# Down projections of a two-layer decoder trunk: three of the seven block products accumulate onto the first one's PSUM banks

## The chip, the cores and the metric

The kernel runs on one core of one Trainium2 chip. The metric is the device time of one execution in microseconds (us); the median of three runs of the kernel before is 2087.05 us (2086.24 to 2087.7).

## The reference, cut to what matters

The model is a trunk of two layers over 1024 tokens with 1024 features, all in float32: a short gated convolution with a feed-forward block, then latent attention with a feed-forward block, and a last RMS norm. The change touches the second half of both feed-forward blocks, the down projection with the 2816 x 1024 matrix `w2`, and the operands that are made for it:

```python
def swiglu_ffn(h, w13, w2):
    g, u = jnp.split(h @ w13, 2, axis=-1)
    return (jax.nn.silu(g) * u) @ w2
...
h = h + swiglu_ffn(rms_norm(h, conv_ffn_norm_g[i]), conv_ffn_w13[i], conv_ffn_w2[i])
...
h = h + swiglu_ffn(rms_norm(h, mla_ffn_norm_g[j]), mla_ffn_w13[j], mla_ffn_w2[j])
```

## The kernel before, in words

Every matrix product splits its two operands into a high and a low part (`split`, L109: ScalarE casts to the high part, VectorE subtracts it to get the low part) and multiplies high by high, high by low and low by high (`three`, L152): three matmuls, lines 153, 154 and 155, per tile of 128 x 128 weights and 512 tokens. In the profile the matmul of L153 reads `mp_hi` and `wp_hi`, that of L154 `mp_lo` and `wp_hi`, that of L155 `mp_hi` and `wp_lo`.

The large products use a Strassen scheme with seven block products in place of eight. For the down projection (`Down`, L658) the contraction (22 chunks of 128) and the output features (8 blocks of 128) and the tokens (1024) are each cut in half. A product `i` of the seven takes one half-size weight block (read from `w2`, or a sum of such blocks that GpSimd's queue has put into DRAM earlier) and one half-size operand (from `md`, in DRAM). It runs over 11 chunks in six groups, five of two chunks and one of one chunk. A step is one chunk: four banks `q` (one per 128 output features), three matmuls each, 12 matmuls. So a product is 11 steps and 132 matmuls, and a down projection is seven products. Two of them run in the kernel, "the first" (L1190) and "the second" (L1701).

For each group there is a load of `m` and of `w` on SyncE's queue (7 or 8 steps ahead) and `parts` (L693), which makes the high and low parts of both: ScalarE `mp_hi`, VectorE `mp_lo`, ScalarE `wp_hi`, VectorE `wp_lo`. `parts` is put two steps ahead of the group's first step (L714). The high tiles share four buffers (`hi_tile`), and so do the low tiles, which holds two groups; a third group's parts wait for the first group's matmuls.

The result `st.h` has 8 blocks of features and two halves of tokens; the four pairs of halves are written (cb, t). Each product has a list of outputs with signs in the table `SEVEN` (L647): after the product, `evict` (L738) adds or subtracts each bank into each listed part of `st.h`, one VectorE instruction of 128 x 512 from PSUM (line 740). There are 14 such pairs in the table, 4 instructions each. They are spread two to a step over the steps that follow the product (`s + j // 2`, L745). `LAST` (L656) names the product after which a part of `st.h` is final, and two steps later `complete` hands it to what follows.

The order of work is written out by hand: `Steps` (L266) holds the steps, and what is put before or after a step is emitted there. Within an engine's queue that is the order of execution. What is put after a step is emitted ahead of what is put before the next one. Each product allocates four of PSUM's eight banks in its first step, so a product's banks were last read by the additions of the product two places earlier.

In the first down projection VectorE also computes the rotary tables (`tables`, L1112, one small piece per step; the profile calls their tiles `rot`), and in its last products `raw_parts` (L1168) splits the finished parts of `st.h`. In the second one `finish` (L1641) squares and scales the finished parts, and the last product is done in halves of 256 tokens.

Before the down projection, `ffn_quads` (L1007) makes the seven operands from pairs of blocks; `right` (L1034) makes operand 6 and `corner` (L1042) makes operand 4 with VectorE subtractions of 128 x 512 (line 1047).

Of the kernel before, what the change touches and what calls it, by code (L numbers as in the profile page):

```python
# [13 lines left out]
ALU = mybir.AluOpType  # L14
# [34 lines left out]
def trunk(ctx, tc, aps, out):  # L49
    nc = tc.nc  # L50
# [199 lines left out]
    class Stream:  # L250


        def __init__(self):
            self.h = [None] * KD
            self.acc = None
# [282 lines left out]
    def complete(n, t, final, keep=True):  # L538

        final(n, t)  # L540
        if t and keep:
            nc.sync.dma_start(hd[n], st.h[n])
# [89 lines left out]
    class Kept:  # L632
# [11 lines left out]

    SEVEN = (  # L647
# [7 lines left out]
    )  # L655
    LAST = {(0, 0): 3, (1, 0): 4, (0, 1): 5, (1, 1): 6}  # L656

    class Down:  # L658


        def __init__(self, steps, m, ws, nk, w, final, keep=True, half=None):

            self.by_half = half
            self.m, self.ws, self.half, self.final, self.keep = m, ws, nk // 2, final, keep
            self.groups = [list(range(a, min(a + 2, self.half))) for a in range(0, self.half, 2)]
            self.wv = w.rearrange("(k p) n -> p k n", p=P)
            self.ends = []
            for i in range(7):
                self.product(steps, i)

        def product(self, steps, i):
            wb, mb, outs = SEVEN[i]
            banks, tail = [], []
            for g, ks in enumerate(self.groups):
                n = len(ks) * 512
                box = {}

                def load_m(box=box, ks=ks, n=n):
                    box["m"] = slot("m")[:, :n]
                    nc.sync.dma_start(box["m"].rearrange("p (k t) -> p k t", t=512),  # L680
                                      self.m[mb - 1, ks[0]:ks[-1] + 1].rearrange("k p t -> p k t"))

                def load_w(box=box, g=g, ks=ks, n=n):
                    r = box["w"] = raw_tile("w2")[:, :n]
                    if isinstance(wb, int):
                        nc.sync.dma_start(r, self.ws[wb, g][:, :n])
                    else:
                        cb, kb = wb
                        k = kb * self.half + ks[0]
                        nc.sync.dma_start(r.rearrange("p (k m) -> p k m", m=512),  # L690
                                          self.wv[:, k:k + len(ks), cb * 512:(cb + 1) * 512])

                def parts(box=box, n=n):  # L693
                    for key in ("m", "w"):
                        hi, lo = hi_tile(key + "p_hi")[:, :n], lo_tile(key + "p_lo")[:, :n]
                        split(hi, lo, box[key])
                        box[key + "p"] = (hi, lo)

                def one(c, q, ts=slice(0, 512), box=box, ks=ks):
                    if not banks:  # L700
                        banks.extend(ps1("dn") for _ in range(4))
                    k = ks[c]
                    (mh, ml), (wh, wl) = box["mp"], box["wp"]
                    cs, ws = slice(c * 512 + ts.start, c * 512 + ts.stop), slice(c * 512 + q * P, c * 512 + (q + 1) * P)
                    more = {"skip_group_check": True} if ts.start else {}
                    three(banks[q][:, ts], wh[:, ws], wl[:, ws], mh[:, cs], ml[:, cs], k == 0, k == self.half - 1, **more)

                s = len(steps.pe)
                if i == 0 and g == 0:
                    self.start = s  # L710
                    steps.before(s, lambda: load_h((4, 5, 6, 7, 0, 1, 2, 3)))
                steps.before(max(s - 8, self.start + 2) if g == len(self.groups) - 1 else s - 8, load_m)
                steps.before(s - 7, load_w)
                steps.before(s - (1 if tail else 2), parts)  # L714
                if i == 6 and g >= len(self.groups) - 2:
                    tail += [lambda q, *ts, c=c, one=one: one(c, q, *ts) for c in range(len(ks))]
                    continue
                for c in range(len(ks)):
                    s = steps.add(lambda c=c, one=one: [one(c, q) for q in range(4)])
            if tail and self.by_half:  # L720
                halves = [slice(th * 256, (th + 1) * 256) for th in range(2)]

                def add(q, th):
                    hv = st.h[4 + q][:, 512:][:, halves[th]]
                    nc.vector.tensor_tensor(hv, hv, banks[q][:, halves[th]], ALU.add)

                for th in range(2):
                    for q in range(4):
                        s = steps.add(lambda q=q, th=th: [fn(q, halves[th]) for fn in tail])
                        steps.after(s, lambda q=q, th=th: self.by_half(q, th, lambda: add(q, th)))  # L730
                self.ends.append(s)
                return
            for q in range(4 if tail else 0):
                s = steps.add(lambda q=q: [fn(q) for fn in tail])
            self.ends.append(s)
            todo = [(q, *o) for q in range(4) for o in outs]

            def evict(q, cb, t, sign):  # L738
                hv = st.h[cb * 4 + q][:, t * 512:(t + 1) * 512]
                nc.vector.tensor_tensor(hv, hv, banks[q], ALU.add if sign > 0 else ALU.subtract)  # L740
                if LAST[cb, t] == i and tail:
                    complete(cb * 4 + q, t, self.final, self.keep)

            for j, o in enumerate(todo):
                n = s - 3 + o[0] if tail else s + j // 2  # L745
                steps.after(n, lambda o=o: evict(*o))
                if LAST[o[1], o[2]] == i and not tail:
                    steps.after(n + 2, lambda o=o: complete(o[1] * 4 + o[0], o[2], self.final, self.keep))

    class Norm:  # L750

# [255 lines left out]
    def ffn_quads(w13, m):  # L1007
        wv = w13.rearrange("a k n -> (a k) n").rearrange("(k p) n -> p k n", p=P)

        first = {}  # L1010

        def store(i, j, t):
            nc.sync.dma_start(m[i - 1, j], t)

        def one(j):

            last, j0, box = j >= KF // 2, j % (KF // 2), {}

            def product(c1, c2):
                nc.vector.tensor_tensor(c1, c1, c2, ALU.mult)  # L1020
                store(2 if last else 1, j0, c1[:, :512])
                if last:
                    store(3, j0, c1[:, 512:])
                    box["b"] = [(c[:, :512], c[:, 512:]) for c in (first.pop(j0), c1)]
                else:
                    first[j] = c1

            def left(c1, c2):
                (b11, b12), (b21, b22) = box["b"]
                box["s"] = work("msum")  # L1030
                box["t1"], box["t2"] = box["s"][:, :512], box["s"][:, 512:]
                sub(5, box["t1"], b12, b11)

            def right(c1, c2):  # L1034
                (b11, b12), (b21, b22) = box["b"]
                sub(6, box["t2"], b22, box["t1"])

            def low(c1, c2):
                (b11, b12), (b21, b22) = box["b"]
                sub(7, b12, b22, b12)  # L1040

            def corner(c1, c2):  # L1042
                (b11, b12), (b21, b22) = box["b"]
                sub(4, b21, box["t2"], b21)

            def sub(i, o, x, y):
                nc.vector.tensor_tensor(o, x, y, ALU.subtract)
                store(i, j0, o)

            done = [product, left, right, low, corner] if last else [product]  # L1050
            return Quad(wv, j * P, DFF + j * P, AF.Silu, done, nc.vector)

        return [one(j + f) for j in range(KF // 2) for f in (0, KF // 2)]
# [48 lines left out]
    e = pl.ends  # L1102
# [92 lines left out]
    for j, fn in enumerate(turns_[0] + turns_[1]):  # L1195
        steps.before(dn.start + 6 + j, fn)
    for j in range(4):
        steps.before(e[3] + 3 + 2 * j, lambda n=j: raw_parts(n, 0))
        steps.before(e[4] + 3 + 2 * j, lambda n=j + 4: raw_parts(n, 0))
        steps.before(e[5] + 3 + 2 * j, lambda n=j: raw_parts(n, 1))  # L1200


# [548 lines left out]
```

## Time and profile before

| | value |
|---|---|
| median of three runs | 2087.05 us |
| the profiled execution's own time | 2084.46 us |
| its span, first to last instruction | 2082.7 us |
| TensorE matmul busy | 98 % of the span |
| VectorE busy | 70 % |
| ScalarE busy | 41 % |
| mean granted TensorE clock | 0.999 of full speed |
| first down projection | 771 to 985 us |
| second down projection | 1852 to 2072 us |

A matmul's row lasts longer than its share of the pipeline: consecutive matmuls start closer together than one lasts. So a lost moment on TensorE is read from the distance between two starts, not from a busy share. In the timeline a row gives the start, the duration, the engine, the line, the operation and its tiles; a bracket at its end gives the idle time before it and what ended that time.

### The profile page before, as it was taken

What the parts mean: (1) busy time and instruction counts of PE and PEld (TensorE: products, weight loads), DVE (VectorE), ACT (ScalarE), POOL (GpSimd) and SP (SyncE); (2) the same over time, 40 slices, a digit from 0 to 9 for tenths busy, and PEclk for the clock granted to TensorE, in tenths of its full rate; (3) what the DMA queues carried; (4) which work ended last, traced back from release to release, by engine and by line L of the source; (5) the groups of instructions that cost most, each with busy time, mean ns of one, the idle gap of its engine ahead of it and who ended that gap; (6) DMA issues with size and microseconds to landing.
All of it is one profiled execution on the core that took longest, in us unless ns stands there. A gap on an engine that the chain in (4) does not pass through costs nothing.

```text
span 2082.7 us, 25559 instructions
## 1 busy us (share of the span) xinstructions
PE 2050.6 (98%) x9542; PEld 1701.2 (82%) x9542; DVE 1463.8 (70%) x2201; ACT 855.4 (41%) x1441; POOL 267.4 (13%) x388
## 2 busy tenths in 40 slices
PE   7999999999999999999999999999999999999998
PEld 6888888888888887787788888788888888888887
DVE  5996666787666667967577777637986666667555
ACT  7533434533333333354345545325533333333355
POOL 1111100121121210000023222110111111100000
PEclk9999999999999999999999999999999999999999
DMA  7255765596766687554332213525487475686543
GB/s 236 81 135 138 237 240 174 118 215 182 190 162 158 145 267 269 197 207 143 87 74 69 53 56 92 190 86 179 135 199 180 147 171 151 153 301 219 182 167 127
DMA packets 274317, 338.98 MB, mean 163 GB/s; under 512 B 18047, under 2 KB 177984, under 8 KB 273872
## 3 DMA queue, kind: packets, MB, share of 16 engines
q1 hardware_dynamic: 240144, 262.71, 38.8%
q0 software_dynamic: 33888, 74.56, 16.7%
q8 instruction: 75, 1.23, 0.2%
q14 instruction: 50, 0.41, 0.1%
q10 hardware_dynamic: 160, 0.07, 0.0%
HBM read 260.22 MB, written 126.35 MB: 186 GB/s over the span
## 4 chain that ended last, share of the span: by engine, by line
PE 88%; DVE 6%; ACT 3%; issue 2%; DMA 2%; DVEq 0%; SPq 0%; ACTq 0%
PE q L153 16%; PE q L155 16%; PE q L154 16%; PE dn L155 5%; PE dn L154 5%; PE dn L153 5%; PE ps_s L1480 4%; PE pl L155 2%; PE pl L153 2%; PE pl L154 2%; PE ps_t L1502 1%; DVE wp_lo L112 1%; PE ps_l L155 1%; PE ps_l L153 1%; PE ps_l L154 1%
## 5 line engine op out<-in xcount | busy, mean ns | idle before, releaser
L153 PE MATMUL q<-xh,w_hi 128*128 128x512 f32 x1568 | 612.5, 391 | 0.7 <-ACT c L451 0.4
L154 PE MATMUL q<-xl,w_hi 128*128 128x512 f32 x1568 | 610.6, 389 | 0.7 <-DVE xl L963 0.7
L155 PE MATMUL q<-xh,w_lo 128*128 128x512 f32 x1568 | 610.3, 389 | 0.0
L153 PEld LDWEIGHTS q<-xh,w_hi 128*128 128x128 f32 x1568 | 294.3, 188 | 63.8 <-ACT xh L959 0.9
L154 PEld LDWEIGHTS q<-xl,w_hi 128*128 128x128 f32 x1568 | 294.4, 188 | 63.0 <-DVE xl L963 1.9
L155 PEld LDWEIGHTS q<-xh,w_lo 128*128 128x128 f32 x1568 | 294.3, 188 | 61.1
L112 DVE TENSOR_TENSOR w_lo<-wr,w_hi 128x512 fp32r<-128x512 f32 (+1 forms) x272 | 191.9, 706 | 199.6 <-ACT w_hi L111 197.8
L111 ACT CAST w_hi<-wr 128x512 fp32r<-128x512 f32 (+1 forms) x272 | 170.1, 629 | 292.6 <-DVE wr L390 196.2
L155 PE MATMUL dn<-mp_hi,wp_lo 128*128 128x512 f32 (+1 forms) x628 | 244.0, 388 | 2.5 <-DVE wp_lo L112 0.8
L153 PE MATMUL dn<-mp_hi,wp_hi 128*128 128x512 f32 (+1 forms) x628 | 242.8, 387 | 0.0
L154 PE MATMUL dn<-mp_lo,wp_hi 128*128 128x512 f32 (+1 forms) x628 | 242.1, 386 | 0.0
L1083 POOL COPY paced<-pace 128x1 f32<-128x1 f32 x128 | 73.0, 570 | 999.7 <-ACT pace L1082 999.7
L112 DVE TENSOR_TENSOR mp_lo<-m,mp_hi 128x1024 fp32r<-128x1024 f32 x84 | 95.3, 1135 | 120.4 <-ACT mp_hi L111 120.4
L111 ACT CAST mp_hi<-m 128x1024 fp32r<-128x1024 f32 x84 | 82.2, 978 | 222.0 <-PE dn L154 211.9
L155 PEld LDWEIGHTS dn<-mp_hi,wp_lo 128*128 128x128 f32 x628 | 117.9, 188 | 32.6 <-DVE wp_lo L112 9.4
L154 PEld LDWEIGHTS dn<-mp_lo,wp_hi 128*128 128x128 f32 x628 | 118.0, 188 | 23.6
L153 PEld LDWEIGHTS dn<-mp_hi,wp_hi 128*128 128x128 f32 x628 | 118.0, 188 | 23.2 <-DVE h L740 0.2
L112 DVE TENSOR_TENSOR wp_lo<-w,wp_hi 128x1024 fp32r<-128x1024 f32 x84 | 94.8, 1129 | 0.0
L473 ACT ACTIVATE c<-c 128x512 f32<-128x512 f32 x44 | 27.8, 633 | 131.9 <-DVE c L448 131.9
L111 ACT CAST wp_hi<-w 128x1024 fp32r<-128x1024 f32 x84 | 81.7, 972 | 0.0
L382 DVE TENSOR_TENSOR w_lo<-wr,w_hi 128x1024 fp32r<-128x1024 f32 x56 | 68.3, 1219 | 12.9 <-ACT w_hi L378 7.9
L1487 ACT ACTIVATE p<-ps_s,mx,rq 128x128 f32<-128x128 f32 (+3 forms) x64 | 53.2, 833 | 53.1 <-DVE mx L1484 47.9
(296 smaller groups left out, 3227.7 us busy)
## 6 DMA issues: line engine op xcount, KB each, us to landing
m<-md_f SPq DMA_DIRECT2D x70, 512.0 KB, 4.8
md_f<-c SPq DMA_DIRECT2D x110, 256.0 KB, 3.7
wr<-in_conv_ffn_w_dram SPq DMA_DIRECT2D x47, 512.0 KB, 6.6
wr<-in_mla_ffn_w_dram SPq DMA_DIRECT2D x47, 512.0 KB, 5.5
w<-mw_f SPq DMA_DIRECT2D x40, 512.0 KB, 3.8
h<-hd SPq DMA_DIRECT2D x32, 512.0 KB, 9.0
wr<-in_conv_w_in_dram SPq DMA_DIRECT2D x31, 512.0 KB, 5.9
mw_f<-in_conv_ffn_w_dram POOLq DMA_DIRECT2D x30, 512.0 KB, 7.5
```

What stands on the lines that cost most here:

```text
L111: nc.scalar.copy(out=hi, in_=src)
L112: (eng or nc.vector).tensor_tensor(lo, src, hi.bitcast(F32), ALU.subtract)
L153: nc.tensor.matmul(ps, lhsT=wh, rhs=xh, start=st, stop=False, **more)
L154: nc.tensor.matmul(ps, lhsT=wh, rhs=xl, start=False, stop=False, **more)
L155: nc.tensor.matmul(ps, lhsT=wl, rhs=xh, start=False, stop=en, **more)
L382: nc.vector.tensor_tensor(lo, self.ra, hi.bitcast(F32), ALU.subtract)
L473: nc.scalar.activation(self.C1[:, 512:], self.C1[:, 512:], self.first)
L1083: nc.gpsimd.tensor_copy(b, a)
L1480: nc.tensor.matmul(ps[:, a:b], lhsT=q[:, qs], rhs=k[:, a:b], start=i == 0, stop=i == 4)
L1487: nc.scalar.activation(p[:, :kw], ps[:, :kw], AF.Exp, bias=mx, scale=rq[:, qb:qb + 1], accum_out=rsum)
L1502: nc.tensor.transpose(t[:, j * P:(j + 1) * P], ps_[j][:, kb * P:(kb + 1) * P], ident)
```

## The change

The table `SEVEN` gets a new order and a flag. Products 2, 3 and 4 (the third, fourth and fifth in time) accumulate on top of product 0 in the same four banks: they take over the list of banks that product 0 left in `self.chain` and don't start a new accumulation. Product 1 runs between product 0 and product 2 in four other banks, products 5 and 6 have banks of their own. Because a bank now holds the sum of product 0 and of those that follow it, each of the first five products has a single output, product 5 has two and product 6 one: eight pairs in place of fourteen, 32 additions per down projection in place of 56. After products 2 and 3 all four additions are emitted right after the last step (`s`), after the others two to a step as before. Operands 4 and 6 change their sign for it; `corner` uses `scalar_tensor_tensor` in place of `tensor_tensor`. `LAST` and the order of `raw_parts` follow the new table: part (1, 0) is final after product 1, part (0, 0) after product 4. The parameters `lag` and `ahead` have the values 2 and 8 that stood there as constants.

```diff
     SEVEN = (
-        ((1, 0), 1, ((1, 0, 1), (1, 1, 1), (0, 0, -1), (0, 1, -1))),
-        (1, 6, ((1, 1, -1), (0, 0, 1), (0, 1, 1))),
-        (3, 7, ((0, 0, -1), (0, 1, -1))),
-        ((0, 1), 4, ((0, 0, -1),)),
-        ((1, 1), 2, ((1, 0, 1),)),
-        (0, 5, ((1, 1, -1), (0, 1, 1))),
-        (2, 3, ((1, 1, 1),)),
+        ((1, 0), 1, False, ((1, 0, 1),)),
+        ((1, 1), 2, False, ((1, 0, 1),)),
+        (1, 6, True, ((1, 1, 1),)),
+        (3, 7, True, ((0, 1, -1),)),
+        ((0, 1), 4, True, ((0, 0, -1),)),
+        (0, 5, False, ((1, 1, -1), (0, 1, 1))),
+        (2, 3, False, ((1, 1, 1),)),
     )
-    LAST = {(0, 0): 3, (1, 0): 4, (0, 1): 5, (1, 1): 6}
+    LAST = {(1, 0): 1, (0, 0): 4, (0, 1): 5, (1, 1): 6}
...
-            wb, mb, outs = SEVEN[i]
-            banks, tail = [], []
+            wb, mb, onto, outs = SEVEN[i]
+            banks, tail = self.chain if onto else [], []
+            if i == 0:
+                self.chain = banks
...
-                    more = {"skip_group_check": True} if ts.start else {}
-                    three(banks[q][:, ts], wh[:, ws], wl[:, ws], mh[:, cs], ml[:, cs], k == 0, k == self.half - 1, **more)
+                    more = {"skip_group_check": True} if ts.start or onto else {}
+                    three(banks[q][:, ts], wh[:, ws], wl[:, ws], mh[:, cs], ml[:, cs], k == 0 and not onto,
+                          k == self.half - 1, **more)
...
-                n = s - 3 + o[0] if tail else s + j // 2
+                n = s - 3 + o[0] if tail else s if i in (2, 3) else s + j // 2
...
-                sub(6, box["t2"], b22, box["t1"])
+                sub(6, box["t2"], box["t1"], b22)
...
-                sub(4, b21, box["t2"], b21)
+                nc.vector.scalar_tensor_tensor(b21, box["t2"], -1.0, b21, ALU.mult, ALU.subtract)
+                store(4, j0, b21)
...
-        steps.before(e[3] + 3 + 2 * j, lambda n=j: raw_parts(n, 0))
-        steps.before(e[4] + 3 + 2 * j, lambda n=j + 4: raw_parts(n, 0))
+        steps.before(e[3] + 3 + 2 * j, lambda n=j + 4: raw_parts(n, 0))
+        steps.before(e[4] + 3 + 2 * j, lambda n=j: raw_parts(n, 0))
```

## Rows read from the trace of the kernel before

**Rows 1.** The page: busy time of each engine (PEld: TensorE's weight loads) with its share of the span and number of instructions, and the granted clock in 40 slices, in tenths.

```profile
PE 2050.6 (98%) x9542; PEld 1701.2 (82%) x9542; DVE 1463.8 (70%) x2201; ACT 855.4 (41%) x1441; POOL 267.4 (13%) x388
...
PEclk9999999999999999999999999999999999999999
```

**Rows 2.** The page: the chain that ended last, shares of the span by engine.

```profile
PE 88%; DVE 6%; ACT 3%; issue 2%; DMA 2%; DVEq 0%; SPq 0%; ACTq 0%
```

**Rows 3.** The instructions that touch the tile `dn` (the banks of both down projections): number, shortest, median and longest duration in ns; then who ended idle time ahead of them (us in total, times).

```profile
L153 PE MATMUL dn<-mp_hi,wp_hi x628: 278/389/482, 771.0 to 2071.5; 128*128 128x512 f32 x151, 128*128 128x256 f32 x6
...
L740 DVE TENSOR_TENSOR h<-h,dn x108: 677/680/690, 803.0 to 2047.9; 128x512 f32<-128x512 f32 x108
...
  DVE wp_lo L112: 10.2, 20
...
  DVE h L740: 0.2, 1
```

**Rows 4.** VectorE in the stretch 770 to 990 us, groups by line and shape: number, busy us, mean ns of one, idle us before them.

```profile
L112 DVE TENSOR_TENSOR mp_lo<-m,mp_hi 128x1024 fp32r<-128x1024 f32 x34 | 41.6, 1223 | 39.1 <-ACT mp_hi L111 39.1
L112 DVE TENSOR_TENSOR wp_lo<-w,wp_hi 128x1024 fp32r<-128x1024 f32 x34 | 41.4, 1218 | 0.0
L740 DVE TENSOR_TENSOR h<-h,dn 128x512 f32<-128x512 f32 x55 | 35.1, 681 | 0.1
L1137 DVE SCALAR_TENSOR_TENSOR rot<-rot 128x512 f32<-128x512 f32 x24 | 16.5, 686 | 0.1
...
L1047 DVE TENSOR_TENSOR msum<-c,msum 128x512 f32<-128x512 f32 x1 | 0.7, 686 | 0.0
```

**Rows 5.** ScalarE's timeline: the cast that opens the preparation of the next product's first group, ahead of the change from product 2 to product 3 of the first down projection.

```profile
860.94 1.05 ACT L111 CAST mp_hi<-m 128x1024 fp32r<-128x1024 f32 x1 [4.30 <-PE dn L154]
```

**Rows 6.** TensorE's timeline: the first matmuls of products 0 and 1 of the first down projection; the first four of its product 3; the first of its product 4; the first of products 3 and 4 of the second down projection.

```profile
770.98 0.39 PE L153 MATMUL dn<-mp_hi,wp_hi 128*128 128x512 f32 x1
...
800.89 0.39 PE L153 MATMUL dn<-mp_hi,wp_hi 128*128 128x512 f32 x1
...
863.69 0.39 PE L153 MATMUL dn<-mp_hi,wp_hi 128*128 128x512 f32 x1
863.91 0.39 PE L154 MATMUL dn<-mp_lo,wp_hi 128*128 128x512 f32 x1
864.44 0.50 PE L155 MATMUL dn<-mp_hi,wp_lo 128*128 128x512 f32 x1
864.78 0.39 PE L153 MATMUL dn<-mp_hi,wp_hi 128*128 128x512 f32 x1
...
894.04 0.39 PE L153 MATMUL dn<-mp_hi,wp_hi 128*128 128x512 f32 x1
...
1942.76 0.39 PE L153 MATMUL dn<-mp_hi,wp_hi 128*128 128x512 f32 x1
...
1973.13 0.39 PE L153 MATMUL dn<-mp_hi,wp_hi 128*128 128x512 f32 x1
```

**Rows 7.** VectorE's timeline at the same four changes of product (2 to 3 and 3 to 4 in the first, then in the second down projection); where a row holds several instructions, its duration is from the first one's start to the last one's end.

```profile
862.02 1.23 DVE L112 TENSOR_TENSOR mp_lo<-m,mp_hi 128x1024 fp32r<-128x1024 f32 x1 [3.48 <-ACT mp_hi L111]
863.17 1.22 DVE L112 TENSOR_TENSOR wp_lo<-w,wp_hi 128x1024 fp32r<-128x1024 f32 x1
864.30 1.41 DVE L1137 SCALAR_TENSOR_TENSOR rot<-rot 128x512 f32<-128x512 f32 x2
865.63 1.28 DVE L740 TENSOR_TENSOR h<-h,dn 128x512 f32<-128x512 f32 x2
...
894.77 0.42 DVE L1153 TENSOR_SCALAR rot<-rot 64x512 f32<-64x512 f32 x1
895.23 1.28 DVE L740 TENSOR_TENSOR h<-h,dn 128x512 f32<-128x512 f32 x2
...
1943.37 1.28 DVE L740 TENSOR_TENSOR h<-h,dn 128x512 f32<-128x512 f32 x2
...
1946.84 2.47 DVE L740 TENSOR_TENSOR h<-h,dn 128x512 f32<-128x512 f32 x4
...
1973.74 1.28 DVE L740 TENSOR_TENSOR h<-h,dn 128x512 f32<-128x512 f32 x2
```

**Rows 8.** Who waited for whom among TensorE's weight loads in 803 to 831 us (first row, inside product 1) and in 834 to 862 us (second row, inside product 2): us in total, times, longest. Then TensorE's timeline at the longest of these places, its weight load first.

```profile
PEld dn L155 <- DVE wp_lo L112: 1.0, 2, 0.5
...
PEld dn L155 <- DVE wp_lo L112: 1.5, 2, 0.8
...
850.40 0.19 PEld L155 LDWEIGHTS dn<-mp_hi,wp_lo 128*128 128x128 f32 x1 [0.78 <-DVE wp_lo L112]
...
849.65 0.39 PE L154 MATMUL dn<-mp_lo,wp_hi 128*128 128x512 f32 x1
850.40 0.50 PE L155 MATMUL dn<-mp_hi,wp_lo 128*128 128x512 f32 x1 [0.36 <-DVE wp_lo L112]
850.74 0.39 PE L153 MATMUL dn<-mp_hi,wp_hi 128*128 128x512 f32 x1
```

**Rows 9.** The longest wait of TensorE for VectorE, at the kernel's start (TensorE's timeline), and the two stretches around and after it (us, then busy us and number of TensorE's matmuls, its weight loads, VectorE, ScalarE and GpSimd, then the granted clock, the DMA share and GB/s).

```profile
13.09 0.67 PE L949 MATMUL xps<-ident,xt 128*128 128x128 f32 x3 [2.20 <-DVE xt L921]
...
10.00:15.00 5.00, 2.63 (x21) 2.06 (x20) 4.39 (x13) 3.25 (x6) 1.66 (x2) 1.00 1.11 359
15.00:20.00 5.00, 4.03 (x17) 2.12 (x15) 3.68 (x7) 4.59 (x8) 0.00 (x0) 1.00 1.02 401
```

More of the change, by code (lines that the diff above doesn't have):

```diff
@@ L647, in trunk, with __init__ @@
     SEVEN = (
[7 rows of a table removed]
+        ((1, 0), 1, False, ((1, 0, 1),)),
[5 more added lines that the diff above has]
+        (2, 3, False, ((1, 1, 1),)),
     )
-    LAST = {(0, 0): 3, (1, 0): 4, (0, 1): 5, (1, 1): 6}
+    LAST = {(1, 0): 1, (0, 0): 4, (0, 1): 5, (1, 1): 6}
     class Down:
-        def __init__(self, steps, m, ws, nk, w, final, keep=True, half=None):
+        def __init__(self, steps, m, ws, nk, w, final, keep=True, half=None, lag=2, ahead=8):
+            self.lag, self.ahead, self.chain = lag, ahead, None
             self.by_half = half
@@ L711, in product @@
                     steps.before(s, lambda: load_h((4, 5, 6, 7, 0, 1, 2, 3)))
-                steps.before(max(s - 8, self.start + 2) if g == len(self.groups) - 1 else s - 8, load_m)
+                steps.before(max(s - self.ahead, self.start + 2) if g == len(self.groups) - 1 else s - self.ahead, load_m)
                 steps.before(s - 7, load_w)
@@ L744, in product @@
             for j, o in enumerate(todo):
-                n = s - 3 + o[0] if tail else s + j // 2
+                n = s - 3 + o[0] if tail else s if i in (2, 3) else s + j // 2
                 steps.after(n, lambda o=o: evict(*o))
                 if LAST[o[1], o[2]] == i and not tail:
-                    steps.after(n + 2, lambda o=o: complete(o[1] * 4 + o[0], o[2], self.final, self.keep))
+                    steps.after(n + self.lag, lambda o=o: complete(o[1] * 4 + o[0], o[2], self.final, self.keep))
     class Norm:
```

## The prediction

> **What bounds the kernel now.** I read the page first. TensorE is busy for 98% of the span, its granted clock is at full speed in every slice [rows 1], and it makes up 88% of the chain that ended last [rows 2]. So the time is the number of matmuls by the distance of their starts, plus the moments in which TensorE has to wait. The change leaves the matmuls alone, and takes work from VectorE. That is worth something only where TensorE waits for VectorE today, and it costs something where TensorE will have to wait anew.
>
> Next I asked who waits at the banks of the down projections. In both together TensorE's idle time is put down to the split `wp_lo` twenty times, and to the additions (line 740) once, for 0.2 us [rows 3]. So the additions are not waited for directly; they stand in VectorE's queue ahead of splits that are. Then I went through TensorE's starts. Between the first matmuls of products 0 and 1 lie 800.89 - 770.98 = 29.91 us for 132 matmuls, 0.227 us each [rows 6]; a larger distance is lost time.
>
> Two kinds of loss come out. The first is at the change of product. The new product's third matmul, L155, starts 0.53 us after the second and the next one 0.34 us after that, which loses 0.53 + 0.34 - 2 x 0.227 = 0.42 us [rows 6]; 0.11 of it is the second distance, a slow restart. The reason is the buffers. The last group has one chunk, one step of 2.7 us. Only when TensorE has left the group before it does ScalarE begin the casts (860.94, after a wait for a matmul) [rows 5]; VectorE's two splits follow at 862.02 and 863.17, and the second ends at 864.39, 0.05 us before L155 starts [rows 6, 7]. VectorE was idle for 3.48 us ahead of them [rows 7], so fewer additions don't bring them forward: this loss stays at every change of product.
>
> The second kind is inside products 1 and 2 of the first down projection, where additions, rotary pieces and splits pile up: four waits of the weight load of L155, 1.0 + 1.5 us [rows 8]. At the longest the load waits 0.78 us and the starts lose 0.75 + 0.34 - 0.45 = 0.64, so 0.14 less. In all 2.5 - 4 x 0.14 = 1.9 us are lost. In the second down projection, without rotary pieces, I find none of this kind.
>
> **What the change removes.** 24 additions per down projection, 48 in all. Four in a row take 2.47 us and one takes 0.68, so they start (2.47 - 0.68)/3 = 0.60 us apart [rows 3, 7]: some 29 us of VectorE, nearly all beside TensorE's work. What is worth time is the pile-up: product 0 leaves 4 additions in place of 16, product 1 leaves 4 in place of 12. I take all 1.9 us as gained; the lower end is 0, should rotary pieces and splits alone be late.
>
> **What it adds.** Product 3 writes onto banks from which product 2's partial sum must first be read, with nothing between the two products, and product 4 onto those of product 3: two handovers per down projection. The new wait stands at the first matmul of each bank. Behind it on TensorE is the whole next product, and behind that ScalarE's next casts, which wait for buffers. When is the addition of bank 0 done? VectorE takes its work in the order written: splits of the next product's first group (put ahead of the last step), rotary pieces, and only then the additions (put after the last step). Today's rows show that order [rows 7].
>
> - First down projection, 2 to 3: the addition starts at 865.63, ends 0.68 later, and with the 0.05 us from above the matmul starts at 866.36 in place of 863.69, 2.67 us late. Add 0.11 for the restart and take off the 0.42, which the longer wait covers: +2.36. Two rotary pieces (1.41 us, from 864.30) stand ahead of it.
> - 3 to 4: 895.23 + 0.73 = 895.96 against 894.04: 1.92 + 0.11 - 0.42 = +1.61. Here one rotary piece is ahead, at 894.77.
> - Second down projection, 2 to 3: 1943.37 + 0.73 = 1944.10 against 1942.76: 1.34 + 0.11 - 0.42 = +1.03.
> - 3 to 4: 1973.74 + 0.73 = 1974.47 against 1973.13, also +1.03, from the same rows [rows 6, 7].
>
> The sum is 6.0 us. Banks 1 to 3 add nothing: the additions follow 0.60 us apart, TensorE takes 3 x 0.227 = 0.68 us per bank. Nor does the next group: its splits now follow four additions, from 865.63 + 3 x 0.60 + 0.68 = 868.1 and end 1.15 + 1.22 later at 870.5, while TensorE needs them 24 matmuls and two after its restart, at 866.36 + 0.11 + 26 x 0.227 = 872.4. No row shows a matmul that waits for an addition of its own bank, so bounds: from below 0 each (the addition is done in time, and the 0.42 stays), from above the same figures plus 3 x 0.60 = 1.8 each, if all four additions had to be done. I take bank 0's own, as the additions are one instruction per bank.
>
> A rule speaks against the change here. The Trainium skill (PSUM — Partial Sum Buffer, "PSUM bank collisions raise a hardware error") says that TensorE and VectorE may not touch one bank at the same moment, and that a bank, not an address, is to be guarded. By the trace alone, where line 740 holds TensorE for 0.2 us in 108 additions, the handover would cost nothing; by the rule it costs the full wait. No run here shows a bank refilled while it is read, since today the banks alternate.
>
> Another rule would make it cheaper: the Trainium skill (TensorE: Matmul & The Clock Gate, the table of specifications at its head) say that TensorE's queue pulls weight loads ahead of matmuls in flight. Then the 0.11 us of restart would fall away at a handover, where weights are ready, and the sum would be 0.44 us less. At today's change of product the weights themselves are late [rows 6], so no row here decides it.
>
> **What costs nothing.** The subtraction that becomes `scalar_tensor_tensor` takes 686 ns in that form on 128 x 512 and 686 as it is [rows 4], 22 times. The signs change no count. Products 1 to 3 load other operands and weights in a new order, as many and as far ahead; each is needed no earlier than it was made before. The finishing of (1, 0) moves from product 4 to product 2, that of (0, 0) from product 3 to product 4, where the other one stood: same work in the same kind of place, and no wait on it in either [rows 3]. Product 5 finds the four banks of product 1, free since early in product 2.
>
> **The sum.** 6.0 - 1.9 = +4.1 us. The profiled execution took 2084.46 us (its span of 2082.7 and 1.8 around it), and would take 2088.6; the median of the runs was 2.6 us above that execution, and carried onto it the forecast is 2087.05 + 4.1 = 2091.2 us. That is +0.2%, and 0.2% (4.2 us) is about what a measurement of this kernel can tell from no change.
>
> **The rivals.**
> - The handover is hidden, and the kernel is not slower. Its place is VectorE's queue at the end of products 2 and 3, its price the whole 6.0 us, and it decides by whether bank 0's addition ends before product 3's first matmul is due: it would have to start by 863.69 - 0.73 = 862.96. VectorE has idle time until 862.02 [rows 7], and bank 0's last matmul is some 9 x 0.227 = 2.0 us before the end, so there is room; against it is the order written, splits first. Then the gain is left: 2087.05 - 1.9 = 2085.2 us.
> - Each bank's wait costs a restart of its own, 0.11 us for three more banks at four handovers: +1.3, 2092.5 us. For it: three more waits are really added. Against it: they should have been met by 0.1 to 0.3 us.
> - All four additions must be done first: four times 1.8, +7.2, 2098.4 us. Against it: separate banks.
> - The idle time lowers the clock. The longest would be some 2.5 us. The longest wait for VectorE today is 2.20 us, with the granted clock at full speed around and after it [rows 9]. If one group of 24 matmuls (5.4 us) ran at half speed after each of the two long waits, +10.9 us: 2102 us.
> - Product 5 is given the chain's banks: a further handover per down projection, at some +1.0 for its first banks and more for those whose additions stand after a step. 2093 us or above. Today's allocation at the same point, with two additions still to come, shows no such wait [rows 3].
> - It doesn't do what it says in time: VectorE's relief, some 29 us, speeds TensorE or later stages in a way no row shows: below 2083 us.
>
> **How the numbers follow.** The forecast as worked out has 0.62, with a range of its own from 2089.7 to 2092.7 us (the 0.44 below, the gain at half its size above, and the runs' own spread of about 0.7). The hidden handover 0.14, restarts per bank 0.12, all four additions 0.02, the clock 0.02, product 5's banks 0.03, unseen relief 0.05. The range is 2085.0 to 2094.0 us: it takes in the first two rivals and leaves out the others and some of the tails, about 0.17. The limit of 0.2% is at 2091.2, in the middle of the forecast: half of 0.62, most of the restarts, and the rivals above give 0.48 for slower; the other half and most of the hidden handover give 0.45 for no change; 0.07 are left for faster.
>
> **What would show it.** At the starts of products 3 and 4 the first matmul (L153) should wait for line 740, about 2.7, 1.9, 1.3 and 1.3 us late, and L155's wait for `wp_lo` be gone there; at the other changes of product it should stay at 0.42. Inside products 1 and 2 of the first down projection the four waits should be gone. Line 740 should have 60 instructions in place of 108. If no matmul waits for line 740, or additions run ahead of the splits, the step on VectorE's order is wrong; if the waits have other lengths, the terms are.

## The result, and the profile after

The changed kernel takes 2091.3 us in the median of eight runs (2090.02 to 2095.18); the kernel before, run beside it on the same chip, takes 2085.72 us (2082.94 to 2087.7, eight runs). The ratio is 1.0034, with an interval of 1.0025 to 1.0043: slower by 7.1 us, between 5.2 and 9.0. The two medians alone lie 5.6 us apart and the two means 6.6, both inside that interval. The forecast was slower by 4.1 us. That the predicted time, 2091.2 us, lies so close is chance: it stood on the median shown of before, 2087.05 us, 1.3 us above that of this comparison. What counts is the difference, and the forecast made it 3 us too small.

The profiled execution is the slowest of the eight, 2095.18 us with a span of 2092.3 us. Some 3 us of it were lost in the kernel's first 60 us, in code that the change doesn't touch: the mean granted clock there was 0.94 in place of 1.00, and the first down projection begins at 773.9 us in place of 770.98 [rows 6]. I leave these out and read the down projections alone.

The page after: busy times, the granted clock in 40 slices, and the chain of waits, shares of the span by engine.

```profile
PE 2056.2 (98%) x9542; PEld 1708.0 (82%) x9542; DVE 1436.7 (69%) x2153; ACT 857.8 (41%) x1441; POOL 267.6 (13%) x388
...
PEclk9999999999999999999999999999999999999999
...
PE 90%; DVE 4%; ACT 3%; DMA 2%; issue 1%; POOL 0%; DVEq 0%; SPq 0%; ACTq 0%
```

VectorE lost 48 instructions and 27.1 us of work against [rows 1], and its share of the chain fell from 6% to 4% [rows 2]. Read alone, this would look like a gain. TensorE's side shows what was paid. Who waited for whom on TensorE: matmuls in the first down projection, then in the second; last the weight loads in the first (us in total, times, longest).

```profile
PE dn L153 <- DVE h L746: 4.5, 2, 2.6
...
PE dn L153 <- DVE h L746: 2.6, 2, 1.3
...
PEld dn L155 <- DVE wp_lo L112: 2.7, 5, 0.6
```

Line 746 is line 740 of before. Four times the first matmul of a product waits for an addition, 7.1 us in all, where before 108 additions held TensorE for 0.2 us [rows 3]; line 746 has 60 instructions, as forecast. The weight loads' waits for `wp_lo` are five in place of eleven in this down projection: four late splits inside products 1 and 2 are gone [rows 8], and two at the changes 2 to 3 and 3 to 4 are covered by the longer wait. VectorE's timeline at the first handover, then its additions at the third:

```profile
862.97 1.23 DVE L112 TENSOR_TENSOR mp_lo<-m,mp_hi 128x1024 fp32r<-128x1024 f32 x1 [3.97 <-ACT mp_hi L111]
864.11 1.22 DVE L112 TENSOR_TENSOR wp_lo<-w,wp_hi 128x1024 fp32r<-128x1024 f32 x1
865.24 1.41 DVE L1144 SCALAR_TENSOR_TENSOR rot<-rot 128x512 f32<-128x512 f32 x2
866.57 2.48 DVE L746 TENSOR_TENSOR h<-h,dn 128x512 f32<-128x512 f32 x4
...
1952.04 2.47 DVE L746 TENSOR_TENSOR h<-h,dn 128x512 f32<-128x512 f32 x4
```

The order is that of [rows 7]: two splits, two rotary pieces, then the additions, now four in a row. Product 2's last matmul starts at 864.40, so VectorE begins the first addition 2.2 us later. TensorE's timeline at this handover, with the matmuls after it; then at the other three:

```profile
864.40 0.39 PE L155 MATMUL dn<-mp_hi,wp_lo 128*128 128x512 f32 x1
867.40 0.51 PE L153 MATMUL dn<-mp_hi,wp_hi 128*128 128x512 f32 x1 [2.62 <-DVE h L746]
867.71 0.63 PE L154 MATMUL dn<-mp_lo,wp_hi 128*128 128x512 f32 x1
868.14 0.63 PE L155 MATMUL dn<-mp_hi,wp_lo 128*128 128x512 f32 x1
868.56 0.63 PE L153 MATMUL dn<-mp_hi,wp_hi 128*128 128x512 f32 x1
...
870.70 0.58 PE L155 MATMUL dn<-mp_hi,wp_lo 128*128 128x512 f32 x1
871.12 0.39 PE L153 MATMUL dn<-mp_hi,wp_hi 128*128 128x512 f32 x1
871.34 0.39 PE L154 MATMUL dn<-mp_lo,wp_hi 128*128 128x512 f32 x1
...
901.02 0.47 PE L153 MATMUL dn<-mp_hi,wp_hi 128*128 128x512 f32 x1 [1.86 <-DVE h L746]
...
1952.87 0.47 PE L153 MATMUL dn<-mp_hi,wp_hi 128*128 128x512 f32 x1 [1.28 <-DVE h L746]
...
1984.36 0.47 PE L153 MATMUL dn<-mp_hi,wp_hi 128*128 128x512 f32 x1 [1.29 <-DVE h L746]
```

Two things are to be seen here. The first is the handover. The distance 864.40 to 867.40 is 3.00 us, 2.77 more than the 0.227 of the steady stream; at the others it is 2.02, 1.45 and 1.45 more. The second matmul follows 0.31 us behind, a restart of 0.08. With the 0.42 taken off that stood there before, the four cost 2.43 + 1.68 + 1.11 + 1.11 = 6.3 us.

The second is what comes after. From 867.71 to 871.12 the starts are 0.42 to 0.43 us apart, eight distances in 3.41 us where 8 x 0.227 = 1.8 would do, and then all is as before. That is 1.6 us lost in which TensorE waits for nobody. The stretches behind the four handovers show what goes with it (us; busy us and number of TensorE's matmuls, weight loads, VectorE, ScalarE, GpSimd; granted clock, DMA share, GB/s):

```profile
867.00:872.00 5.00, 4.60 (x13) 3.68 (x14) 4.97 (x8) 0.00 (x0) 0.00 (x0) 0.66 0.40 123
901.00:906.00 5.00, 4.98 (x15) 4.00 (x16) 3.94 (x5) 0.34 (x1) 0.00 (x0) 0.66 0.94 307
1952.00:1957.00 5.00, 4.13 (x18) 3.46 (x19) 4.79 (x7) 1.39 (x2) 0.00 (x0) 1.00 0.45 159
1984.00:1989.00 5.00, 4.64 (x20) 3.86 (x21) 4.28 (x6) 0.88 (x1) 0.00 (x0) 1.00 0.46 161
```

The mean granted clock is 0.66 behind the waits of 2.62 and 1.86 us and 1.00 behind the two of 1.28. Taken over 867.7 to 871.1 us alone it is 0.50: the matmuls 0.43 us apart are at the lower of the two levels, 1.2 GHz. The busy share doesn't tell of it: the second stretch is busy for 4.98 of 5.00 us with 15 matmuls, where 5 / 0.227 = 22 would fit. The second fall costs 1.6 us as well. So this profile has 6.3 - 1.9 + 3.2 = +7.6 us. The page's row of the clock shows a 9 in every slice, as before; a fall of the clock for 3.4 us disappears in a slice of 52.

### The profile page after: what moved, and what is told of

It reads as the page before. It is cut to its first block, busy times and chain, and to the rows that moved or that the text cites. A ratio compares the mean times of both kernels' runs of the same rounds, so it can differ in the third digit from the quotient of the medians.

```text
span 2092.3 us, 25519 instructions
## 1 busy us (share of the span) xinstructions
PE 2056.2 (98%) x9542; PEld 1708.0 (82%) x9542; DVE 1436.7 (69%) x2153; ACT 857.8 (41%) x1441; POOL 267.6 (13%) x388
## 3 DMA queue, kind: packets, MB, share of 16 engines
q8 instruction: 74, 1.21, 0.2%
## 4 chain that ended last, share of the span: by engine, by line
PE 90%; DVE 4%; ACT 3%; DMA 2%; issue 1%; POOL 0%; DVEq 0%; SPq 0%; ACTq 0%
PE q L153 16%; PE q L155 16%; PE q L154 16%; PE dn L155 6%; PE dn L153 6%; PE dn L154 6%; PE ps_s L1487 4%; PE pl L155 2%; PE pl L153 2%; PE pl L154 2%; PE ps_t L1509 1%; PE ps_l L155 1%; PE ps_l L153 1%; PE ps_l L154 1%; PE ps_pv L1519 1%
```

## The experiments

Two theories. **A**, the forecast's: the handovers cost their waits, less a gain of 1.9 us, and nothing else; what is above that is chance. **B**: the two long waits also cost TensorE its clock, some 1.6 us each time, and the two short ones don't. Beside them two terms were to be tested alone, the gain and the price of the chain itself. All ratios are against the kernel before on the same chip; 0.001 is 2.1 us.

### The gain alone: fewer additions in the kernel before

```diff
-        ((1, 0), 1, ((1, 0, 1), (1, 1, 1), (0, 0, -1), (0, 1, -1))),
-        (1, 6, ((1, 1, -1), (0, 0, 1), (0, 1, 1))),
-        (3, 7, ((0, 0, -1), (0, 1, -1))),
+        ((1, 0), 1, ((1, 0, 1),)),
+        (1, 6, ((1, 1, -1),)),
+        (3, 7, ((0, 1, -1),)),
```

> The kernel before with six of the fourteen outputs left out of the table (24 additions per down projection left out, the same number that the change saves), no chain of banks. If the four late splits inside products 1 and 2 of the first down projection are all that the additions cost, the time is the one of before minus 1.9 us, about 0.9991 of it, and those four waits are gone. Rival, relief of VectorE is worth more than the trace shows: minus 4 us or more. Rival, rotary pieces and splits alone are late: no difference.

Measured: 2081.86 us against 2083.69, ratio 0.9991 [0.9982, 1.0]. TensorE's weight loads in the first down projection, who waited for whom:

```profile
PEld dn L155 <- DVE wp_lo L112: 3.8, 7, 0.6
```

Seven waits in place of eleven, and 6.2 - 3.8 = 2.4 us less waiting: the four late splits are gone, and those at the changes of product stay. The rows show the gain, and the time has the size that the forecast gave it, though the interval reaches to no gain.

### The chain without its handovers

```diff
-        (1, 6, True, ((1, 1, 1),)),
-        (3, 7, True, ((0, 1, -1),)),
+        (1, 6, True, ()),
+        (3, 7, True, ()),
```

> The changed kernel with the additions after products 2 and 3 left out (8 per down projection), so that the chain of banks stays and nothing has to be read between its products. If the loss is the wait for those additions and the clock that falls after it, the time is the one of before minus 1.9 us, no matmul waits for line 746 at the start of products 3 and 4, the usual 0.42 us per change of product is back there, and the granted clock stays full in both down projections. Rival, accumulating on a used bank or the new order of products costs something by itself: above the time of before.

Measured: 2082.15 us against 2083.69, ratio 0.999 [0.998, 0.9999]. No matmul waits for line 746, the weight loads wait seven times for 3.8 us as in the experiment above, and the changes 2 to 3 and 3 to 4 lose 0.42 each as before. So accumulating on the same banks, the new order of products and the new operands cost nothing by themselves. All that makes the changed kernel slower hangs on the additions between the products.

### Shorter waits: the rotary pieces moved out of the way

```diff
-    for j, fn in enumerate(turns_[0] + turns_[1]):
-        steps.before(dn.start + 6 + j, fn)
+    free = [n for n in range(6, 60) if n not in (31, 32, 42, 43)]
+    for n, fn in zip(free, turns_[0] + turns_[1]):
+        steps.before(dn.start + n, fn)
```

> The changed kernel with the rotary pieces of the first down projection kept out of the two steps ahead of both handovers, so that no piece stands between the splits and the additions. Theory that a wait of 1.9 us or more lets the clock fall and one of 1.3 us does not: the first matmuls of products 3 and 4 wait 1.3 us in both down projections, the granted clock stays full, and the time is the one of before plus 2.5 us (minus 1.9, plus four times 1.45 + 0.08 - 0.42). Rival, the clock falls at the handovers of the first down projection for another reason than the length of the wait: the waits are 1.3 us and the matmuls after them still run at half speed, plus 5.7 us. Rival, the clock costs nothing on top: the gain over the changed kernel is the shorter wait alone, 1.9 us.

Measured: 2087.56 us against 2083.69, ratio 1.0017 [1.0008, 1.0026]. All four waits are now 1.28 us. The first two, and the stretches behind them, in the columns as above:

```profile
866.96 0.47 PE L153 MATMUL dn<-mp_hi,wp_hi 128*128 128x512 f32 x1 [1.28 <-DVE h L746]
...
898.41 0.47 PE L153 MATMUL dn<-mp_hi,wp_hi 128*128 128x512 f32 x1 [1.28 <-DVE h L746]
...
866.00:871.00 5.00, 4.04 (x18) 3.39 (x19) 5.00 (x8) 1.48 (x2) 0.00 (x0) 1.00 0.44 157
898.00:903.00 5.00, 4.58 (x20) 3.85 (x21) 4.97 (x8) 0.94 (x1) 0.00 (x0) 1.00 0.43 157
```

The clock stays at 1.00 at the same two places. By the rows the kernel now loses 4 x 1.11 - 1.9 = 2.5 us; measured were 3.5, between 1.7 and 5.4. Against the changed kernel 3.5 us are won (7.1 - 3.5), of which the shorter waits make up only 1.33 + 0.58 = 1.9: A gives no account of the rest, B does. But the intervals of the two ratios (up to 1.0026, from 1.0025) meet at their ends, so the clock rows speak more plainly here than the times.

### Longer waits in the second down projection

```diff
+    def pad():
+        nc.vector.tensor_tensor(work("pad")[:, :512], st.h[0][:, :512], st.h[1][:, :512], ALU.add)
+
+    steps.before(e[2], pad)
+    steps.before(e[3], pad, pad)
```

> The changed kernel with extra VectorE additions of 128x512 into an unused tile in the second down projection, one ahead of the handover from product 2 to 3 and two ahead of that from 3 to 4. The waits there should be 1.28 + 0.60 = 1.9 and 1.28 + 1.20 = 2.5 us. Theory that the length of the wait decides on the clock: both are followed by some 3.4 us of matmuls at 0.43 us each, the granted clock falls there as in the first down projection, and the kernel is 1.8 + 3.2 = 5.0 us slower than the changed one. Rival, the clock's fall belongs to the first down projection: 1.8 us slower and full clock at these places.

Measured: 2097.27 us against 2083.69, ratio 1.0062 [1.0048, 1.0075], that is 5.8 us beyond the changed kernel's 1.0034, from four runs. TensorE's two waits there, from its timeline:

```profile
1949.64 0.47 PE L153 MATMUL dn<-mp_hi,wp_hi 128*128 128x512 f32 x1 [1.89 <-ACT wp_hi L111]
...
1983.91 0.47 PE L153 MATMUL dn<-mp_hi,wp_hi 128*128 128x512 f32 x1 [2.49 <-DVE h L746]
```

The first is put down to ScalarE's `wp_hi`, but that is the cast of the second group, which this matmul doesn't need. VectorE's first addition begins at 1948.81, behind the pad, and the matmul starts 0.83 us after that, the same step as at the other handovers. The stretches behind all four handovers:

```profile
865.00:870.00 5.00, 4.12 (x18) 3.44 (x19) 5.00 (x8) 0.07 (x1) 0.00 (x0) 1.00 0.44 154
897.00:903.00 6.00, 5.06 (x15) 4.08 (x16) 4.83 (x7) 1.25 (x2) 0.00 (x0) 0.72 0.92 306
1949.00:1954.00 5.00, 4.36 (x12) 3.50 (x13) 4.55 (x6) 0.56 (x1) 0.00 (x0) 0.66 0.47 161
1983.00:1988.00 5.00, 4.08 (x11) 3.25 (x12) 4.83 (x7) 0.23 (x1) 0.00 (x0) 0.66 0.48 159
```

At the two places where the clock was at 1.00 behind 1.28 us, it falls behind 1.89 and 2.49. The waits grew by 0.61 + 1.21 = 1.8 us; with A alone the kernel would be 1.8 us slower than the changed one, with two falls some 5.0. The first row is a surprise: behind its wait of 2.61 us, the longest in this execution, the clock did not fall this time.

### How often: the changed kernel twice more

The kernel as changed, with no edit, twice more: first in five executions, then in a single one.

> The changed kernel unaltered, a second look beside the others. If the clock's fall after the two long waits of the first down projection belongs to the kernel and not to one execution, its profile shows it again at the same two places, and the kernel is 6 to 8 us slower than before. Rival, an accident of the profiled execution: full clock there and some 4.4 us slower.

> The changed kernel unaltered, one more profile, to count how often the granted clock falls. Theory that a wait of 1.86 us or more makes the fall likely and one of 1.28 us does not bring it: at least one of the two handovers of the first down projection is followed by matmuls 0.43 us apart, neither of the second one is. Rival, the fall has nothing to do with the waits: slow matmuls at other places as well.

Measured: 2092.79 us against 2083.89 in the first repeat, ratio 1.0035 [1.0023, 1.0048], which agrees with the result; 2094.26 us in the second. The waits are 2.61, 1.86, 1.28 and 1.28 us in both. The stretches behind the first two, in the first repeat:

```profile
864.00:870.00 6.00, 5.66 (x18) 4.54 (x19) 5.56 (x8) 0.00 (x0) 0.00 (x0) 0.72 0.42 127
898.00:904.00 6.00, 5.95 (x26) 4.96 (x27) 3.97 (x5) 0.77 (x2) 0.00 (x0) 1.00 1.00 299
```

and in the second:

```profile
867.00:872.00 5.00, 3.65 (x16) 3.09 (x17) 5.00 (x7) 0.54 (x1) 0.00 (x0) 1.00 0.49 157
900.00:905.00 5.00, 4.62 (x13) 3.69 (x14) 4.29 (x6) 0.69 (x1) 0.00 (x0) 0.66 0.99 321
```

The same wait is followed by a fall in one execution and not in another. Counted over the four executions with such waits (the first profile of the changed kernel, these two, the one with longer waits): 7 of 10 waits of 1.86 us or more had a fall behind them. Of the ten of 1.28 us (two in each of the first three, four in the rotary experiment) none had.

The other places of the eleven traces that were kept say the same. Behind the first 60 us of the kernel there are 57 single waits of TensorE of 1.0 to 1.7 us, the ten among them, and none has a fall behind it; there are two more of 1.94 and 2.03 us (line 460, a wait for ScalarE), and both have one. So it is 9 of 12 against 0 of 57, and until TensorE has done its last matmul no fall there stands without such a wait. The first 60 us are less simple: in 4 of the 11 executions the clock also fell at 38 us, behind two waits of 0.95 and 0.50 us that follow each other with three small matmuls between.

All executions on record together agree. Each has its mean granted clock on record: it averages 0.9989 over the 72 runs of the kernel before in these experiments (0.997 to 1.000) and 0.9976 over the 14 of the changed one. A fall of 3.4 us to half the clock takes some 0.0008 off a mean over 2090 us, so by an estimate from these numbers the changed kernel has 1.5 falls more per execution; 2 x 0.7 = 1.4 is what the count gives. The four runs with longer waits average 0.9950, the eleven with shorter ones 0.9984; the last is 0.0005 below the kernel before, which their scatter (0.0009 from run to run) doesn't tell from nothing.

### Banks finished in turn, and what it shows of VectorE's queue

Can the chain be kept without its waits? Here products 2 and 3 do the one-chunk group first and finish the last group's banks two by two, so that banks 0 and 1 are added while banks 2 and 3 are still being filled; their additions are put a step earlier.

```diff
+            order = list(enumerate(self.groups))
+            if i in (2, 3):
+                order = order[-1:] + order[:-1]
...
-                steps.before(s - (1 if tail else 2), parts)
+                steps.before(s - (1 if tail or (i in (2, 3) and pos == 1) else 2), parts)
...
+                if i in (2, 3) and pos == len(order) - 1:
+                    for two in ((0, 1), (2, 3)):
+                        s = steps.add(lambda two=two, one=one: [one(c, q) for q in two for c in range(2)])
+                    continue
...
-                n = s - 3 + o[0] if tail else s if i in (2, 3) else s + j // 2
+                n = s - 3 + o[0] if tail else s - 1 + j // 2 if i in (2, 3) else s + j // 2
```

> The changed kernel with another order inside products 2 and 3: the group of one chunk goes first, and in the last group of two chunks the banks are finished one after the other, with the additions of banks 0 and 1 a step ahead of those of banks 2 and 3 and the next splits behind them. If the handover costs only because the additions come late, VectorE reads banks 0 to 2 before the product ends and bank 3 before it is needed 2.0 us into the next product: no matmul waits for line 756, the change from product 3 to 4 loses nothing at all, the clock stays full, and the time is the one of before minus 1.9 and minus twice 0.42, minus 2.7 us. Rival, the additions still stand behind splits that wait for buffers: waits of 1 us or more at some of the four handovers, no faster than before.

Measured: 2082.69 us against 2083.89, ratio 0.9994 [0.9985, 1.0003]: 1.2 us won where 2.7 were expected, with an interval from 3.1 won to 0.6 lost. VectorE's additions (line 753 here) at the first handover:

```profile
858.68 1.28 DVE L753 TENSOR_TENSOR h<-h,dn 128x512 f32<-128x512 f32 x2
...
860.52 0.69 DVE L753 TENSOR_TENSOR h<-h,dn 128x512 f32<-128x512 f32 x1
861.88 0.69 DVE L753 TENSOR_TENSOR h<-h,dn 128x512 f32<-128x512 f32 x1 [0.68 <-PE dn L155]
```

Product 3 begins at 861.68, on bank 0, with no wait: that bank was read by 859.4. The clock is at 1.000 over the whole execution, and no matmul waits for an addition. A part of what is missing stands inside product 2, on VectorE and then on TensorE:

```profile
829.84 1.41 DVE L1151 SCALAR_TENSOR_TENSOR rot<-rot 128x512 f32<-128x512 f32 x2
831.17 1.28 DVE L753 TENSOR_TENSOR h<-h,dn 128x512 f32<-128x512 f32 x2
...
833.66 0.47 PE L154 MATMUL dn<-mp_lo,wp_hi 128*128 128x512 f32 x1
834.77 0.50 PE L155 MATMUL dn<-mp_hi,wp_lo 128*128 128x512 f32 x1 [0.64 <-DVE wp_lo L112]
835.11 0.39 PE L153 MATMUL dn<-mp_hi,wp_hi 128*128 128x512 f32 x1
```

The short group now stands first, so the second group's splits are due one step after it, behind two rotary pieces and two additions: 1.11 + 0.34 - 0.45 = 1.0 us lost, where 0.42 was reckoned with. By the rows 2.2 us should have been won; the times can't tell that from 1.2 or 2.7.

The next version did the short group first in products 1 and 5 as well, to save 0.42 at each of their beginnings too.

```diff
-            if i in (2, 3):
+            if i in (1, 2, 3, 5):
...
-                          k == 0 and not onto,
+                          k == order[0][1][0] and not onto,
...
-                steps.before(s - (1 if tail or (i in (2, 3) and pos == 1) else 2), parts)
+                steps.before(s - (1 if tail or (i == 3 and pos == 1) else 2), parts)
```

> The kernel of the run before (banks finished in turn in products 2 and 3), with two more products, 1 and 5, that begin with the group of one chunk, and the ordinary place for the splits of product 2. Theory that each place where splits of two chunks have to fit into one step loses 0.42 us: there are four such places per down projection in place of six before, and the late splits inside products 1 and 2 of the first one are gone, so the time is the one of before minus 1.9 and minus 4 times 0.42, minus 3.6 us, 0.9983 of it. Rival, rotary pieces or the additions of products 1 and 5 make splits late elsewhere: minus 2.7 us or less.

Measured: 2085.05 us against 2084.47, ratio 0.9997 [0.9988, 1.0006], a miss: 3.6 us were expected. TensorE in the first down projection:

```profile
845.90 0.49 PE L154 MATMUL dn<-mp_lo,wp_hi 128*128 128x512 f32 x1 [0.61 <-DVE mp_lo L112]
847.04 0.50 PE L155 MATMUL dn<-mp_hi,wp_lo 128*128 128x512 f32 x1 [0.64 <-DVE wp_lo L112]
```

The start at 845.90 comes 0.99 us after the one before it, that at 847.04 another 1.14, and the next 0.34 behind: 2.47 - 3 x 0.227 = 1.8 us lost here, and 0.6 at 814.85. VectorE's queue ahead of these splits holds rotary pieces and additions without a gap. In the second down projection, without rotary pieces, nothing of the kind is lost. So the last version keeps this order and moves the pieces away from these steps:

```diff
-    for j, fn in enumerate(turns_[0] + turns_[1]):
-        steps.before(dn.start + 6 + j, fn)
+    free = [n for n in range(6, 60) if n not in (11, 12, 13, 22, 23, 24)]
+    for n, fn in zip(free, turns_[0] + turns_[1]):
+        steps.before(dn.start + n, fn)
```

> The kernel of the run before with the rotary pieces of the first down projection kept out of the first three steps of products 1 and 2. There the profile of that run showed them, with the additions, ahead of the second group's splits, at a loss of 0.6 and 1.8 us. Theory: these two losses go, the first down projection loses 4 times 0.42 and 0.3 us in place of 4.6 before, the second one 3 times 0.42 in place of 5 times: minus 3.5 us, 0.9983 of the time before. Rival: the pieces, pushed six steps back, make splits late in product 4, where parts of the stream are split too: minus 2 us or less, and a late split there.

Measured: 2081.58 us against 2084.91, ratio 0.9985 [0.9976, 0.9994], 3.1 us faster than the kernel before, between 1.3 and 5.0. TensorE's starts lose 0.42 at four places in each down projection, where before it was six in the first and five in the second, and the late splits are gone: 3 x 0.42 + 1.9 = 3.2 us by the rows. By these ratios it beats both kernels, with the change's own idea and its waits taken out. Whether the new order inside the products would help the kernel before as well, without a chain of banks, was not run.

## Why the prediction was right and wrong

**Right: the mechanism of the handover.** The first matmuls of products 3 and 4 wait for line 746, for the reason given: VectorE takes splits, then rotary pieces, then additions. Forecast were 2.67, 1.92, 1.34 and 1.34 us late, measured 2.77, 2.02, 1.45 and 1.45. The term mis-sized by 0.1 each is the step from the addition's start to the matmul's: 0.73 forecast (0.68 and the 0.05 of a split), 867.40 - 866.57 = 0.83 measured. The restart was 0.08 in place of 0.11. Together 6.3 us in place of 6.0. That one wait holds per product and not one per bank shows as well: line 746 ends two waits of a matmul in each down projection, and there are two handovers in each. So neither banks 1 to 3 nor product 5 wait, and the rivals of a hidden handover, of a restart per bank, of all four additions and of product 5's banks fall.

**Right: the gain.** 1.9 us from four late splits; the first experiment gives 1.9 by its ratio (0 to 3.8), and the rows show these four gone. The interval leaves no room for 4 us or more, so the rival of an unseen relief falls too.

**Right: what costs nothing.** New order, operands, chain: the second experiment is 0.999 with all of them in it.

**Wrong: the clock.** The step that failed is the term for the clock: the sum put it at nothing, and the rival "The idle time lowers the clock" had a chance of 0.02. The one row against it, a wait of 2.20 us at the kernel's start with the clock at 1.00 [rows 9], was taken as proof that such a wait is harmless. It was one execution. In 5 of the 11 traces the clock falls at that very wait, in the profile of the changed kernel too: there the wait ends at 14.17 us and the mean clock of 15 to 20 us is 0.72, where [rows 9] have 1.00. In the down projections waits of 1.86 to 2.62 us were followed by a fall in 7 of 10 cases. The price given to the rival was wrong the other way: not a group of 24 matmuls at half speed but eight distances, 1.6 us, each time. On average that is 2 x 0.7 x 1.6 = 2.2 us, and 6.3 - 1.9 + 2.2 = 6.6 us stands well inside the measured 5.2 to 9.0. Without the falls 4.4 us would be below it. That the length of the wait brings the falls is shown by shortening and lengthening it: at the same two places the clock stayed up behind 1.28 us, and at two others it fell when 1.28 became 1.89 and 2.49; the count over all traces, 9 of 12 against 0 of 57, agrees. Why the same wait is followed by a fall in one execution and not in another stays open.

**The two rules weighed.** The Trainium skill (PSUM — Partial Sum Buffer, "PSUM bank collisions raise a hardware error") has a bank guarded as a whole against TensorE and VectorE at once; the trace agrees in so far as each first matmul starts 0.83 us after the start of the addition on its bank, which lasts 0.68: the full wait at all four handovers. Whether a bank or only its addresses are guarded isn't shown, since a matmul and an addition cover the same 128 x 512 numbers here. The Trainium skill (TensorE: Matmul & The Clock Gate, the table of specifications at its head) has weight loads pulled ahead of matmuls in flight; across this wait the trace shows none. ScalarE had cast `wp_hi` by 863.89 us (start 862.84, 1.05 long), yet the loads of the first two weights are:

```profile
867.37 0.19 PEld L153 LDWEIGHTS dn<-mp_hi,wp_hi 128*128 128x128 f32 x1 [3.01 <-ACT wp_hi L111]
867.48 0.19 PEld L154 LDWEIGHTS dn<-mp_lo,wp_hi 128*128 128x128 f32 x1
```

They start when the wait is over, 0.03 us ahead of the first matmul and 0.08 behind it, and the second matmul follows its load by 0.23 us as in the steady stream. So the restart lost 0.08 us, hardly less than the 0.11 of a late weight. The bracket names a cast that had long been done; whether the program or the engine holds the loads back isn't shown.

**The sum.** +4.1 us became +7.1: 0.3 of the difference is the handover's size, some 2.2 the clock (an average over executions), and 0.5 is within the interval. That the time lies within the forecast's 2085.0 to 2094.0 us in spite of the missing term is in part luck: the term was small.

## What to carry to other kernels

A saving on an engine that isn't the bound is worth only the waits of the bound that it removes; a dependency that it adds on the bound's path costs its full distance in the other engine's queue, so look first at what is queued ahead of the instruction that releases it. Where a bank is refilled, let banks finish in turn and read the first while the last is filled, and keep movable work away from the steps where splits or additions are due. Ask of every new wait on TensorE how long it is: in these runs one of 1.0 to 1.7 us cost itself, one of 1.9 or more often cost 1.6 us on top. And don't take one execution for proof that a wait is harmless.

## What the hardware did that I had not expected

A single wait of 1.86 us out of a dense stream of matmuls was enough for TensorE's granted clock to fall to its lower level for some 3.4 us. It came back while the matmuls went on without a pause. It happens in some executions and not in others (9 of 12 waits), and it hardly marks the page: the mean clock of a single run reads 0.996 to 0.999 for the changed kernel and 0.997 to 1.000 for the one before. The average over many runs shows it, and so do the distance of starts and the windows right behind the wait. It isn't VectorE's doing either: in the second repeat of the changed kernel a wait of 1.94 us for ScalarE (line 460), ended at 438.53 us in another product, had matmuls 0.43 us apart from 440.16 on.
